# Differential values and gates as two token-major units of half products

## The chip, the cores and the metric

One of the eight cores of a Trainium2 chip runs the kernel. The number that counts is the device time of one launch in microseconds (us), here the median of three runs. The engines of a core work from their own instruction streams and meet by semaphores: TensorE (PE in the profile) multiplies into PSUM banks of 128 partitions x 512 fp32 values, VectorE (DVE) and ScalarE (ACT) do elementwise work, GpSimd (POOL) and SyncE (SP) mainly issue DMAs here.

## The reference

Two layers over 512 tokens of width 2048, all in float32. This change lies in the second one, which projects the normed x once and shares the columns out to an MLA branch and a differential attention branch:

```
z = rmsnorm(x, g) @ w_in
c_q, c_kv, k_rope, mla_gate, dq, dk, dv, diff_gate = split_cols(z, ODD_SPLITS)   # dv, diff_gate: 1024 each
...
a = p[:, 0] - lam * p[:, 1]                      # two causal softmaxes of one head, 8 heads
od = einsum("bhqk,bkhd->bqhd", a, vd)            # 128 values a head
od = rmsnorm(od, subln) * (1.0 - DIFF_LAMBDA_INIT)
y_d = od.reshape(B, S, DIFF_WIDTH) * jax.nn.silu(diff_gate)
return jnp.concatenate([y_c, y_d], axis=-1) @ w_out
```

## The kernel before

Matrices are multiplied in fp32r, each operand split into a high and a low part: `mm3` issues three matmuls (high x high, high x low, low x high) into one bank. A *row tile* is 128 of the 2048 rows of the contraction, so a job over 16 row tiles is 48 matmuls of 128x512.

Activations lie feature-major: `X1[k]` is the pair (high `sh`, low `sl`) of 128 features x 512 tokens of x times the gain g, made one by one as layer 0's output projection delivers them (`sink0`, which also writes x to `x1d` in HBM). The factor of the rms norm belongs to a token; it is put on when a sum leaves its bank (`evac`, a VectorE product with `rstd`), and the norm `n1` is finished only after the last row tile.

A weight `Piece` is 128 x 1024 floats (512 KB): SP loads it into one of three `wr` slots, ScalarE makes its high part (`wh`), VectorE its low part (`wl`), three slots each. `Piece.want()` is called as TensorE's row reaches a piece and sees to it that the splits of two pieces ahead and the loads of two more are issued. `big_job(wt, m, X, done, pre, norm)` is a job of two pieces into one bank of the pair "mm". The bank pairs "o", "sc" and "pt" serve attention outputs, scores and transposes.

The order on TensorE, ScalarE and VectorE is fixed when the program is built: `Plan` keeps a clock by a cost model, the jobs run in the order in which they were made, and after every step `tick` runs the side tasks (generators with a due time) that are due, which drops their instructions between the matmuls. Each engine works its row in order. SP's and GpSimd's rows follow from the framework's scheduler.

After layer 0 come eight heads of four jobs, `dq`, `dk`, `dv`, `dg` (tiles 4h to 4h+3 of `w1`), then five MLA gate jobs, the latents, the rope key, three more gates, the MLA heads and the output projection. `diff(h)` starts when `dv` has left its bank: it transposes v to token-major by four TensorE transposes (`pt<-cc,dv`), copies it out on ScalarE, and runs scores, softmaxes (`p`), transposes of them (`aT`) and `o`. `diff_gate` puts Silu on the gate, transposes the normed output `osb` and multiplies the two. x's tiles, scores, splits of activations and so on live in a pool of 76 work tiles of 128x512.

Of the kernel before, what the change touches and what calls it, by code (L numbers as in the profile page):

```python
# [9 lines left out]
F32 = mybir.dt.float32  # L10
# [63 lines left out]
class Plan:  # L74
# [82 lines left out]
    def after(self, *aps):  # L157

        return max(self.ready.get(a.tensor.name, 0.0) for a in aps)
# [30 lines left out]


@with_exitstack
def trunk_kernel(ctx: ExitStack, tc, xT, w0, w0o, wg, w1, wuq, wuk, wuv, w1o, small, cst, outT):
    plan = Plan()
    nc = tc.nc
    pe = Engine(plan, "PE", nc.tensor, plan.pe_cost)
# [86 lines left out]
    class Piece:  # L283


        def __init__(self, src, n, kept=False):
# [28 lines left out]
        def want(self):  # L315
            last = len(pieces) - 1
            while state["split"] <= min(self.i + 2, last):
                while state["dma"] <= min(state["split"] + 2, last):
                    pieces[state["dma"]].load()
                    state["dma"] += 1  # L320
                pieces[state["split"]].split()
                state["split"] += 1

        def get(self, off, n):
            h, l = self.parts[off // S]
            return h[:, off % S : off % S + n], l[:, off % S : off % S + n]

    jobs = []

# [608 lines left out]
        yield after(aT)  # L938
        out.append(aT)

    ods = {}

    def diff(h, st):
        t = []
        yield after(st["v"])
        yield from take("pt", t)
        transposes(t[0], st["v"], range(NB))
        yield after(t[0])
        v = wk("v")
        act.activation(v, t[0], AF.Copy)  # L950
        give("pt", t[0])
        q, kt, klow = st["q"], st["kh"], st["kl"]
        st.clear()
# [53 lines left out]
        ods[h] = osb  # L1007

    def diff_gate(h, z):
        while h not in ods:  # L1010
            yield plan.now + 0.5
        act.activation(z, z, AF.Silu)
        osb = ods.pop(h)
        yield after(osb)
        t = []
        yield from take("pt", t)
        transposes(t[0], osb, range(NB))
        yield after(t[0], z)
        dve.scalar_tensor_tensor(z, z, subs, t[0], ALU.mult, ALU.mult)
        give("pt", t[0])  # L1020
        Y1[h] = z

    def diff_jobs(h):
        st = {}

        def q_done(acc):
            z = evac(acc, n1, "dq")
            st["q"] = []
            plan.spawn(stacks(z, st["q"]))

        def k_done(acc):
            z = evac(acc, n1, "dk")
            lo = [wk("kl", F32R), wk("kl", F32R)]
            a = [wk("kh", F32R), wk("kh", F32R)]
            st["kh"], st["kl"] = a, lo

            def f():
                yield after(z)
                for c in range(2):
                    r, s = slice(64 * c, 64 * c + 64), slice(64 - 64 * c, 128 - 64 * c)  # L1040
                    high(a[c][r], z[r])
                    high(a[c][s], z[r])
                    yield after(a[c])
                    low(lo[c][r], z[r], a[c][r])
                    low(lo[c][s], z[r], a[c][r])
            plan.spawn(f())

        def v_done(acc):
            st["v"] = evac(acc, n1, "dv")
            plan.spawn(diff(h, st))  # L1050

        def g_done(acc):
            plan.spawn(diff_gate(h, evac(acc, n1, "dg")))
# [6 lines left out]
    for h in range(8):  # L1060
        diff_jobs(h)

    MG = [None] * 8

    def mla_gate_job(h):
        def done(acc):
            z = evac(acc, n1, "mg")

            def f():
                yield after(z)  # L1070
                act.activation(z, z, AF.Silu)
                MG[h] = z
            plan.spawn(f())
        big_job(w1, 32 + h, X1, done, None, n1)

    class Latent:
        def __init__(self, base, n, gcol):
# [41 lines left out]
            KR.extend((h, l))  # L1119
        plan.spawn(f())  # L1120

    for h in range(5):
        mla_gate_job(h)
    LQ = Latent(45, 6, C_QN)
    LKV = Latent(41, 4, C_KVN)
    big_job(w1, 40, X1, rope_key_done, None, n1)
    for h in range(5, 8):
        mla_gate_job(h)

    qrs = {}  # L1130
    VC = {}
# [49 lines left out]
    def mla(h, st):  # L1181
        while h not in qrs or not KR or "q" not in st or "k" not in st or h != started[0] or (h // 4, NB - 1) not in VC:
            yield plan.now + 0.4
        q, k, qr = st["q"], st["k"], qrs.pop(h)
        st.clear()
        vc = slice((h % 4) * P, (h % 4 + 1) * P)
        v = [VC[h // 4, n] for n in range(NB)]
        o = []
# [190 lines left out]
def _tiles1():  # L1379

    cq, ckv, kr, mg, dq, dk, dv, dg = 0, 768, 1280, 1344, 2368, 3392, 4416, 5440
    out = []
    for h in range(8):
        for b in (dq, dk, dv, dg):
            out.append(_ranges((b + 128 * h, b + 128 * h + 128)))
    for h in range(8):
        out.append(_ranges((mg + 128 * h, mg + 128 * h + 128)))
    out.append(_ranges((kr, kr + 64), (kr, kr + 64)))
    for j in range(4):
        out.append(_ranges((ckv + 128 * j, ckv + 128 * j + 128)))  # L1390
    for j in range(6):
        out.append(_ranges((cq + 128 * j, cq + 128 * j + 128)))
    return out


def _pack(w, tiles, rows=None):
# [7 lines left out]
    return out  # L1404


def _pack_small(w, cols):
# [80 lines left out]
```

## Time and profile before

| | |
|---|---|
| runs | 1565.23, 1565.57, 1565.69 us; median 1565.57 |
| profiled execution | 1567.61 us; its span in the trace 1565.8 us; granted TensorE clock 0.995 |
| busy | TensorE 1549.5 us, VectorE 866.4, ScalarE 705.2, GpSimd 48.2 |
| HBM | 146.49 MB read, 8.39 MB written, 99 GB/s over the span |

Nearly all instructions are recorded at line 62, the wrapper that also feeds the planner's clock, so groups are told apart by the names of the tiles: `mm<-sh,wh` is a matmul into a bank of the pair mm from a high part of x and a high part of a weight; `wl<-wr,wh` is the low part of a weight. "Idle before, releaser" is the engine's own idle time ahead of such instructions and what ended it. In the chain of work that ended last, pieces of one engine follow each other, and what waits for nothing is put to the engine itself.

### The profile page before, as it was taken

To read this page: it belongs to the slowest core of one execution; us is meant where nothing else is said; L and a number is where in the kernel's file an instruction comes from. 1 tells how busy PE (TensorE), PEld (TensorE's weight loads), DVE (VectorE), ACT (ScalarE), POOL (GpSimd) and SP (SyncE) were. 2 spreads that over 40 slices of the span, in tenths; PEclk is the share of its full clock that TensorE was granted. 3 is DMA by queue.
4 is the path that set the end of the run, shared out by engine and by line. 5 is a ranking of instruction groups with operands and counts; after the bars stand their busy time and mean duration, and the time that the engine had idled before them with its cause. 6 is when DMAs were issued, how large, how long until landed. Compare 5 with 4: busy or idle time off the path is not lost.

```text
span 1565.8 us, 19224 instructions
## 1 busy us (share of the span) xinstructions
PE 1549.5 (99%) x7450; PEld 1297.9 (83%) x7450; DVE 866.4 (55%) x1603; ACT 705.2 (45%) x1219; POOL 48.2 (3%) x76
## 2 busy tenths in 40 slices
PE   9999999999999999999999999999999999999996
PEld 7888888888888888888888888888888888888886
DVE  6877676677854344455445555543444465843344
ACT  6465555556643233444445444432323466632222
POOL 0000000000001010000000000000000000010000
PEclk9999999999999999999999999999999999999998
DMA  7223222322244443222222222222232221343323
GB/s 281 84 85 93 86 84 86 97 81 81 95 128 148 135 155 110 91 83 84 90 82 81 81 81 84 92 81 94 95 94 87 78 79 53 115 141 95 101 89 108
DMA packets 48922, 156.11 MB, mean 100 GB/s; under 512 B 5552, under 2 KB 9792, under 8 KB 48704
## 3 DMA queue, kind: packets, MB, share of 16 engines
q1 hardware_dynamic: 44576, 141.25, 28.4%
q0 software_dynamic: 4256, 13.64, 2.7%
q8 instruction: 58, 0.95, 0.3%
q14 instruction: 32, 0.26, 0.1%
HBM read 146.49 MB, written 8.39 MB: 99 GB/s over the span
## 4 chain that ended last, share of the span: by engine, by line
PE 97%; issue 1%; DVE 1%; DMA 0%; SPq 0%; POOLq 0%; ACT 0%; POOL 0%; DVEq 0%
PE mm L62 84%; PE o L62 5%; PE sc L62 5%; PE pt L62 4%; DMA xin<-in_xT 0%; DVE st L62 0%; SPq L62 0%; DVE sl L62 0%; POOLq L1483 0%; ACT sh L62 0%; POOL rcf L62 0%; DVE mg L62 0%; DVE yl L62 0%; DVE dg L62 0%; DVEq L1483 0%
## 5 line engine op out<-in xcount | busy, mean ns | idle before, releaser
L62 PE MATMUL mm<-sh,wh 128*128 128x512 f32 x1312 | 522.5, 398 | 0.0
L62 DVE TENSOR_TENSOR wl<-wr,wh 128x1024 fp32r<-128x1024 f32 (+1 forms) x244 | 290.6, 1192 | 418.3 <-ACT wh L62 418.2
L62 PE MATMUL mm<-sh,wl 128*128 128x512 f32 x1312 | 512.3, 390 | 0.0
L62 PE MATMUL mm<-sl,wh 128*128 128x512 f32 x1312 | 512.0, 390 | 0.0
L62 ACT ACTIVATE wh<-wr 128x1024 fp32r<-128x1024 f32 (+1 forms) x244 | 252.3, 1034 | 402.7 <-PE mm L62 325.1
L62 PEld LDWEIGHTS mm<-sh,wl 128*128 128x128 f32 x1312 | 246.3, 188 | 53.2
L62 PEld LDWEIGHTS mm<-sh,wh 128*128 128x128 f32 x1312 | 246.7, 188 | 45.3
L62 PEld LDWEIGHTS mm<-sl,wh 128*128 128x128 f32 x1312 | 247.1, 188 | 44.7
L62 PE MATMUL mm<-yh,wh 128*128 128x512 f32 x448 | 174.9, 390 | 0.0
L62 PE MATMUL mm<-yl,wh 128*128 128x512 f32 x448 | 174.5, 389 | 0.0
L62 PE MATMUL mm<-yh,wl 128*128 128x512 f32 x448 | 174.4, 389 | 0.0
L62 DVE CUSTOM_DVE_ANT_0 p<-sc,cc 128x128 f32<-128x128 f32 (+3 forms) x96 | 47.0, 490 | 96.6 <-PE sc L62 96.4
L62 PEld LDWEIGHTS mm<-yh,wl 128*128 128x128 f32 x448 | 84.1, 188 | 17.6
L62 PEld LDWEIGHTS mm<-yl,wh 128*128 128x128 f32 x448 | 84.1, 188 | 17.4 <-DVE yl L62 0.3
L62 PEld LDWEIGHTS mm<-yh,wh 128*128 128x128 f32 x448 | 84.1, 188 | 17.1
L62 ACT ACTIVATE p<-p,negm 128x128 f32<-128x128 f32 (+3 forms) x96 | 53.7, 560 | 68.3 <-DVE negm L62 66.8
L62 ACT ACT_TABLE_LOAD x50 | 64.2, 1283 | 1.5 <-PEq L1479 0.7
L62 ACT ACTIVATE aT<-pt 128x128 f32<-128x128 f32 (+3 forms) x64 | 27.7, 436 | 60.1 <-PE pt L62 59.9
L62 ACT ACTIVATE sq<-xr 128x512 f32<-128x512 f32 (+1 forms) x33 | 19.3, 586 | 55.0 <-DVE xr L62 55.0
L62 DVE TENSOR_TENSOR ss<-ss,sq 128x512 f32<-128x512 f32 (+1 forms) x54 | 36.1, 669 | 10.2 <-ACT sq L62 9.4
L62 PE MATMUL mm<-ch,wh 128*128 128x512 f32 x104 | 41.6, 400 | 0.0
L62 PE MATMUL mm<-cl,wh 128*128 128x512 f32 x104 | 40.6, 391 | 0.0
(253 smaller groups left out, 1822.0 us busy)
## 6 DMA issues: line engine op xcount, KB each, us to landing
wr<-in_w SPq DMA_DIRECT2D x166, 512.0 KB, 3.5
wr<-in_w0o SPq DMA_DIRECT2D x32, 512.0 KB, 3.6
wr<-in_w1o SPq DMA_DIRECT2D x32, 512.0 KB, 3.5
wr<-in_wuq SPq DMA_DIRECT2D x12, 384.0 KB, 3.1
xin<-in_xT SPq DMA_DIRECT2D x16, 256.0 KB, 5.2
xr<-in_xT POOLq DMA_DIRECT2D x16, 256.0 KB, 3.8
x1d<-xr POOLq DMA_DIRECT2D x16, 256.0 KB, 3.5
xr<-x1d POOLq DMA_DIRECT2D x16, 256.0 KB, 3.0
```

Of the source, the lines that this page charges most:

```text
L62: return f(*args, **kw)
```

## The change

`dv` and `dg` are no longer jobs of the heads. Each of the two column ranges of 1024 becomes a `Unit`, which computes the whole 512 tokens x 1024 columns token-major: blocks of 128 tokens of x stand still, weights move 512 wide, and a bank holds 128 tokens x 512 columns. Six pairs of row tiles (k and 8+k, twelve of sixteen) are multiplied by seven products of halves, after Strassen in Winograd's form: tokens are halved (256), row tiles are halved by the pairing, columns are halved (512). The sums of x (`T1` to `T4`) are made once by `differences()` from x read back from `x1d`; the sums of weights are made per piece by the class `Sum`, which loads one or two sources, adds on VectorE and then splits. Banks X, Y, Z are the pairs mm, o, sc, two token blocks each. Per pair of row tiles `differences()` issues two fetches by SP, two scalings and two high parts on ScalarE, five half-width differences and two low parts on VectorE. A piece holds two row tiles of one column half. After the first nine pieces (`first`) s1 is copied from X, then s2 = Z + s1 and s3 = Y + s2 are added; `second` lets Z and Y be written anew, `third` makes t = X - s3, `fourth` sends off c11 = Z + s1 and c12 = Y + s3, and the end c21 = X - s2 and c22 = Z + t. The four results leave by a ScalarE scaling with the token's norm factor (Identity for v, Silu for the gate) and a GpSimd DMA to `vd` and `gd` in HBM. The remaining four row tiles are multiplied plainly into the same banks by four ordinary pieces.

The order now is five MLA gate jobs (their results too go through HBM, `mgd`), unit v, unit g, then eight heads of `dq` and `dk` only, which fetch v and g by DMA as `dq` begins; then latents, rope key, three gates and the MLA heads as before. `diff` needs no transposing of v, puts the gate on with the norm (`osb`), and writes y from the transposed output on ScalarE. By the rows TensorE issues 696 matmuls of 128x512 for the two units where 768 stood for the sixteen jobs.

```
+    class Sum(Piece):
+        ahead = 3
...
+        def split(self):
+            vals = self.vals + [o.vals[0] for o in self.others]
+            if len(vals) > 1:
+                out = [wk("ws"), wk("ws")] if self.into is None else vals[self.into]
...
+                    for k in range(2):
+                        dve.tensor_tensor(out[k], vals[0][k], vals[1][k], ALU.add)
...
+                high(h[:, c], v[k])
+                low(l[:, c], v[k], h[:, c])
...
     def diff(h, st):
-        t = []
-        yield after(st["v"])
-        yield from take("pt", t)
-        transposes(t[0], st["v"], range(NB))
-        yield after(t[0])
-        v = wk("v")
-        act.activation(v, t[0], AF.Copy)
-        give("pt", t[0])
-        q, kt, klow = st["q"], st["kh"], st["kl"]
+        q, kt, klow, v, gate = (st[x] for x in ("q", "kh", "kl", "v", "g"))
...
-            dve.tensor_scalar(osb[:, c], o[:, c], ssq[:, n : n + 1], None, ALU.mult)
+            dve.scalar_tensor_tensor(osb[:, c], o[:, c], ssq[:, n : n + 1], gate[:, c], ALU.mult, ALU.mult)
...
-        act.activation(z, z, AF.Silu)
...
-        dve.scalar_tensor_tensor(z, z, subs, t[0], ALU.mult, ALU.mult)
+        y = wk("y")
+        act.activation(y, t[0], AF.Identity, scale=subs)
...
+        def fetch():
+            for x, src in (("v", vd), ("g", gd)):
+                st[x] = wk(x)
+                pool.dma_start(st[x], src[h])
...
-        big_job(w1, 4 * h, X1, q_done, None, n1)
-        big_job(w1, 4 * h + 1, X1, k_done, None, n1)
-        big_job(w1, 4 * h + 2, X1, v_done, None, n1)
-        big_job(w1, 4 * h + 3, X1, g_done, None, n1)
+        big_job(w1, 2 * h, X1, q_done, fetch, n1)
+        big_job(w1, 2 * h + 1, X1, k_done, None, n1)
...
+    NT = 6
+    def differences():
...
+    class Unit:
+        def __init__(self, wt, sink):
...
+            for i in range(n):
+                p1 = Sum([W(0, 0, i)])
+                p5 = Sum([W(1, 0, i), W(1, 1, i)], wide=False)
+                p6 = Sum([], (p5, p1), None)
+                seq += [(p1, "X", "B11", i), (p5, "Y", "T1", i), (p6, "Z", "T2", i)]
+            seq.append(self.first)
+            for i in range(n):
+                seq.append((Sum([W(0, 0, i), W(1, 0, i)], (), 1), "X", "T3", i))
+                if i < 2:
+                    if i == 0:
+                        seq.append(self.second)
+                    seq.append((Piece(W(0, i, 3), 1024), "ZY", None, i))
+            seq.append(self.third)
+            for i in range(n):
+                p2 = Sum([W(0, 1, i)])
+                p3 = Sum([], (self.keep[i], p2), 0)
+                seq += [(p2, "Z", "B21", i), (p3, "Y", "B22", i)]
+            seq.append(self.fourth)
+            for i in range(n):
+                seq.append((Sum([W(1, 1, i)], (), 0, i % 2 == 0), "X", "T4", i))
+            seq.append(self.fifth)
+            for i in range(2):
+                seq.append((Piece(W(1, i, 3), 1024), "XZ", None, i))
...
+    for h in range(5):
+        mla_gate_job(h, True)
+    Unit(w1u[0], away(vd, AF.Identity))
+    Unit(w1u[1], away(gd, AF.Silu))
+    for h in range(8):
+        diff_jobs(h)
```

TensorE in a differential head, before: the four transposes of v stand between the matmuls of the `dg` job, ahead of the head's scores.

```order
L62 MATMUL mm_994_5283<-sl_840_4285,wh_984_5211 128x512
L62 MATMUL mm_994_5283<-sh_839_4284,wl_985_5213 128x512
L62 MATMUL pt_999_5307<-cc_2_78,dv_998_5293 128x128 x4
L62 MATMUL mm_994_5283<-sh_850_4356,wh_984_5211 128x512
L62 MATMUL mm_994_5283<-sl_851_4357,wh_984_5211 128x512
L62 MATMUL mm_994_5283<-sh_850_4356,wl_985_5213 128x512
L62 MATMUL mm_994_5283<-sh_861_4428,wh_984_5211 128x512
```

The same engine in a head after: between the matmuls of `dq` or `dk` (`mm_1392` is one of these) stand scores of one head, the transposes of the output `osb` of another and output products (`o`) of a third, and no row transposes v.

```order
L62 MATMUL mm_1392_7368<-sh_948_5005,wl_1376_7292 128x512
L62 MATMUL sc_1421_7494<-kh_1400_7385,qa_1369_7249 128x256
L62 MATMUL sc_1421_7494<-kl_1398_7383,qa_1369_7249 128x256
L62 MATMUL pt_1424_7500<-cc_2_78,osb_1415_7469 128x128 x4
L62 MATMUL o_1344_7178<-v_1282_6906,aT_1423_7498 128x128 x3
L62 MATMUL sc_1426_7512<-kh_1401_7386,qb_1370_7250 128x256
L62 MATMUL sc_1426_7512<-kl_1399_7384,qb_1370_7250 128x256
```

The transposes of v are gone, and attention work of several heads is mixed. VectorE around the `dv` job, before: low parts of weights (`wl`), the last head's `osb` and gate product, and the eviction of `dv`.

```order
L62 TENSOR_SCALAR ssq_1002_5321<-ssq_1002_5321 128x4
L62 TENSOR_TENSOR kl_1062_5601<-dk_1060_5598,kh_1064_5603 64x512 x2
L62 TENSOR_SCALAR osb_1069_5643<-o_1001_5320,ssq_1002_5321 128x128 x4
L62 TENSOR_TENSOR wl_1073_5661<-wr_1054_5548,wh_1072_5659 128x1024
L62 SCALAR_TENSOR_TENSOR dg_1023_5398<-dg_1023_5398,subs_92_361,pt_1070_5652 128x512
L62 TENSOR_TENSOR wl_1077_5693<-wr_1066_5605,wh_1076_5691 128x1024
L62 TENSOR_TENSOR dv_1078_5698<-mm_1065_5604,rstd_971_5137 128x512
L62 ISA p_1086_5732,negm_1083_5727<-sc_1085_5729,cc_2_78 128x128
```

VectorE in unit v, after the first nine pieces: the low part of a plain piece, a sum of two loads and its low parts (`wx`, `wl_1109`), then the four additions that empty the banks sc (Z) and o (Y).

```order
L62 TENSOR_TENSOR wl_1104_5746<-wr_1087_5666,wh_1103_5744 128x1024
L62 TENSOR_TENSOR wx_1091_5690<-wr_1090_5688,wx_1091_5690 128x512
L62 TENSOR_TENSOR wx_1092_5691<-wr_1090_5688,wx_1092_5691 128x512
L62 TENSOR_TENSOR wl_1109_5769<-wx_1091_5690,wh_1108_5768 128x512
L62 TENSOR_TENSOR wl_1109_5769<-wx_1092_5691,wh_1108_5768 128x512
L62 TENSOR_TENSOR s2_1110_5780<-sc_1070_5592,s1_1105_5760 128x512
L62 TENSOR_TENSOR s3_1111_5788<-o_1065_5571,s2_1110_5780 128x512
L62 TENSOR_TENSOR s2_1112_5790<-sc_1071_5593,s1_1106_5762 128x512
L62 TENSOR_TENSOR s3_1113_5792<-o_1066_5572,s2_1112_5790 128x512
```

The additions stand behind the split of a piece that is used only later. TensorE in the same place of unit v: the end of the first `T3` piece in the banks mm, and the first plain piece, which begins anew in the banks sc that those additions read.

```order
L62 MATMUL mm_1055_5538<-wh_1098_5720,tl_991_5201 128x512
L62 MATMUL mm_1056_5539<-wh_1098_5720,th_988_5185 128x512
L62 MATMUL mm_1056_5539<-wl_1099_5721,th_988_5185 128x512
L62 MATMUL mm_1056_5539<-wh_1098_5720,tl_991_5201 128x512
L62 MATMUL sc_1070_5592<-wh_1103_5744,sh_861_4431 128x512
L62 MATMUL sc_1070_5592<-wl_1104_5746,sh_861_4431 128x512
L62 MATMUL sc_1070_5592<-wh_1103_5744,sl_862_4432 128x512
L62 MATMUL sc_1071_5593<-wh_1103_5744,sh_861_4431 128x512
```

Where a job had one bank for 48 matmuls, the bank now changes every three, and sc is written again one piece after its last product.

More of the change, by code (lines that the diff above doesn't have):

```diff
@@ L317, in want @@
             while state["split"] <= min(self.i + 2, last):
-                while state["dma"] <= min(state["split"] + 2, last):
+                while state["dma"] <= min(state["split"] + self.ahead, last):
                     pieces[state["dma"]].load()
@@ L1071, in f @@
                 act.activation(z, z, AF.Silu)
-                MG[h] = z
-            plan.spawn(f())
-        big_job(w1, 32 + h, X1, done, None, n1)
+                if away:
+                    yield after(z)
+                    pool.dma_start(mgd[h], z)
+                else:
+                    MG[h] = z
+            plan.spawn(f())
+        j = big_job(w1, 16 + h, X1, done, None, n1)
+        if h == 0:
+            j.pre = lambda: plan.spawn(differences())
+    NT = 6
+    TS = [None] * NT
@@ new lines, in differences, with fetch @@
+    def differences():
+        A, B = slice(0, 256), slice(256, 512)
+        def fetch(k):
+            xa, xb = wk("xa"), wk("xb")
+            sync.dma_start(xa, x1d[k])
+            sync.dma_start(xb, x1d[8 + k])
+            return xa, xb
+        nxt = fetch(0)
+        for k in range(NT):
+            xa, xb = nxt
+            if k + 1 < NT:
+                nxt = fetch(k + 1)
+            yield after(xa, xb)
+            act.activation(xa, xa, AF.Identity, scale=col(C_G1 + k))
+            act.activation(xb, xb, AF.Identity, scale=col(C_G1 + 8 + k))
+            yield after(xa, xb)
+            t13, t42 = wk("ta"), wk("tb")
+            dve.tensor_tensor(t13[:, A], xa[:, A], xa[:, B], ALU.subtract)
+            dve.tensor_tensor(t42[:, A], xb[:, A], xb[:, B], ALU.subtract)
+            dve.tensor_tensor(t13[:, B], xa[:, B], xb[:, B], ALU.subtract)
+            dve.tensor_tensor(t42[:, A], t42[:, A], t13[:, A], ALU.subtract)
+            dve.scalar_tensor_tensor(t42[:, B], t13[:, A], -1.0, xb[:, B], ALU.mult, ALU.subtract)
+            yield after(t42)
+            r = []
+            for t in (t13, t42):
+                h = wk("th", F32R)
+                high(h, t)
+                r.append(h)
+            yield after(*r)
+            for i, t in enumerate((t13, t42)):
+                l = wk("tl", F32R)
+                low(l, t, r[i])
+                r[i] = r[i], l
+            TS[k] = r
@@ new lines, in trunk_kernel, with operand, run, order @@
+    class Unit:
+        def __init__(self, wt, sink):
+            self.wt, self.sink, self.pre = wt, sink, None
+            W = lambda m, kh, i: wt[m, kh, i]
+            n = NT // 2
+            seq = []
+            self.keep = []
+            for i in range(n):
+                p1 = Sum([W(0, 0, i)])
+                p5 = Sum([W(1, 0, i), W(1, 1, i)], wide=False)
+                p6 = Sum([], (p5, p1), None)
+                self.keep.append(p6)
+                seq += [(p1, "X", "B11", i), (p5, "Y", "T1", i), (p6, "Z", "T2", i)]
[17 more added lines that the diff above has]
+                seq.append((Piece(W(1, i, 3), 1024), "XZ", None, i))
+            self.seq = seq
+            jobs.append(self)
+        def operand(self, name, k, b):
+            c = slice(b * P, b * P + P)
+            d = slice(256 + b * P, 256 + b * P + P)
+            if name == "B11":
+                x = X1[k], c
+            elif name == "B21":
+                x = X1[8 + k], c
+            elif name == "B22":
+                x = X1[8 + k], d
+            else:
+                plan.until(lambda: TS[k] is not None)
+                x = TS[k][name in ("T2", "T4")], c if name in ("T1", "T4") else d
+            (h, l), c = x
+            return h[:, c], l[:, c]
+        def run(self):
+            if self.pre:
+                self.pre()
+            self.banks = {}
+            self.tags = {}
+            self.begun = set()
+            self.done = set()
+            self.vals = {x: [None] * 2 for x in ("s1", "s2", "s3", "t", "c11", "c12", "c21", "c22")}
+            for s in self.seq:
+                if callable(s):
+                    s()
+                    continue
+                pc, where, name, i = s
+                for x, tag in zip("XYZ", self.order()):
+                    if x in where and x not in self.banks:
+                        plan.until(lambda: len(banks[tag]) == 2)
+                        self.banks[x], self.tags[x] = [bank(tag), bank(tag)], tag
+                pc.want()
+                for j in range(2):
+                    if name:
+                        todo = [(where, b, self.operand(name, 2 * i + j, b)) for b in range(2)]
+                    else:
+                        k = 8 * i + 6 + j
+                        plan.until(lambda: X1[k] is not None)
+                        todo = [(where[n // 2], n % 2, tuple(p[:, n * P : n * P + P] for p in X1[k])) for n in range(4)]
+                    for x, b, (xh, xl) in todo:
+                        out = self.banks[x][b]
+                        mm3(out, xh, xl, pc.get(j * S, S), (x, b) not in self.begun, False)
+                        self.begun.add((x, b))
+                    plan.tick()
+            self.last()
+            plan.tick()
+        def order(self):
+            return ("mm", "o", "sc")
+        def steps(self, name, *ops):
+            def f():
+                for b in range(2):
+                    for op in ops:
+                        yield from op(b)
+                self.done.add(name)
+            plan.spawn(f())
+        def wait(self, *names):
+            plan.until(lambda: all(x in self.done for x in names))
+        def combine(self, out, x, y, op, sign=ALU.add):
+            def f(b):
+                p, q = self.banks[x][b], self.vals[y][b]
+                yield after(p, q)
+                r = q if op else wk(out)
+                dve.tensor_tensor(r, p, q, sign)
+                self.vals[out][b] = r
+            return f
+        def leave(self, out, m, tokens):
+            def f(b):
+                z = self.vals[out][b]
+                plan.spawn(self.sink(m, 2 * tokens + b, z))
+                yield plan.now
+            return f
+        def free(self, x):
+            def f(b):
+                give(self.tags[x], self.banks[x][b])
+                yield plan.now
+            return f
+        def first(self):
+            def copy(b):
+                p = self.banks["X"][b]
+                yield after(p)
+                self.vals["s1"][b] = wk("s1")
+                act.activation(self.vals["s1"][b], p, AF.Copy)
+            self.steps("s1", copy)
+            self.wait("s1")
+            self.begun -= {("X", 0), ("X", 1)}
+            self.steps("s3", self.combine("s2", "Z", "s1", False), self.combine("s3", "Y", "s2", False))
+        def second(self):
+            self.wait("s3")
+            self.begun -= {("Z", 0), ("Z", 1), ("Y", 0), ("Y", 1)}
+        def third(self):
+            self.steps("t", self.combine("t", "X", "s3", False, ALU.subtract))
+        def fourth(self):
+            self.wait("t")
+            self.steps("top", self.combine("c11", "Z", "s1", True), self.leave("c11", 0, 0),
+                       self.combine("c12", "Y", "s3", True), self.leave("c12", 0, 1), self.free("Y"))
+        def fifth(self):
+            self.wait("top")
+            self.begun -= {("Z", 0), ("Z", 1)}
+        def last(self):
+            self.steps("end", self.combine("c21", "X", "s2", True, ALU.subtract), self.free("X"),
+                       self.leave("c21", 1, 0), self.combine("c22", "Z", "t", True), self.free("Z"),
+                       self.leave("c22", 1, 1))
```

79 lines of the change are left out of this document (54 added, 25 removed).

## The prediction

> **What bounds the kernel now.** I read the head of the page first, then the chain of work that ended last.
>
> ```profile
> span 1565.8 us, 19224 instructions
> PE 1549.5 (99%) x7450; PEld 1297.9 (83%) x7450; DVE 866.4 (55%) x1603; ACT 705.2 (45%) x1219; POOL 48.2 (3%) x76
> PE 97%; issue 1%; DVE 1%; DMA 0%; SPq 0%; POOLq 0%; ACT 0%; POOL 0%; DVEq 0%
> ```
>
> TensorE is busy in all of the span and is 97% of the chain, so time goes away only where TensorE gets fewer instructions, and comes back only where it has to wait. The profiled run took 1567.61 us for this span; the median of the runs shown is 1565.57 (1565.23 to 1565.69), 2.04 lower. I sum against 1567.6 and take 2.0 off at the end. Next the chain in two windows, for the pace of TensorE at the turn of the layers and for one differential head:
>
> ```profile
> 554.88 61.43 PE mm L62 x271
> ...
> 647.69 0.44 PE pt L62 x4
> ...
> 649.51 0.24 PE sc L62 x2
> ...
> 689.16 0.44 PE pt L62 x4
> ...
> 698.46 0.44 PE pt L62 x4
> ```
>
> The first row is the pace: 61.43/271 = 0.2267 us for one 128x512 matmul. 647.69 is the transposing of one head's v (four blocks, 0.44 us), and 698.46 the next head's: a head takes 50.77 us, of which four jobs of 48 matmuls are 43.53, the v transposes 0.44 and its attention and output transposes the other 6.80. 649.51 is the head's first score and 689.16 the transposing of its finished output, 39.7 us later. Then windows, to see whether that pace depends on who else works:
>
> ```profile
> 12.00:16.00 4.00, 4.00 (x13) 3.13 (x13) 3.83 (x6) 4.00 (x8) 0.00 (x0) 0.66 1.05 404
> 0.00:20.00 20.00, 16.23 (x62) 12.97 (x63) 11.57 (x19) 13.37 (x22) 2.06 (x8) 0.91 0.92 336
> 20.00:40.00 20.00, 20.00 (x90) 16.57 (x89) 15.80 (x32) 14.33 (x27) 0.00 (x0) 1.00 0.56 213
> 360.00:380.00 20.00, 20.00 (x94) 16.68 (x93) 19.18 (x30) 11.03 (x19) 0.00 (x0) 1.00 0.29 85
> 620.00:1040.00 420.00, 420.00 (x2028) 350.33 (x2028) 218.30 (x449) 196.44 (x374) 10.55 (x7) 1.00 0.27 84
> 1240.00:1300.00 60.00, 60.00 (x322) 51.68 (x321) 35.36 (x86) 36.01 (x74) 0.00 (x0) 1.00 0.22 65
> ```
>
> The columns after the window are its length and the busy time of TensorE, its weight loads, VectorE, ScalarE and GpSimd, then the granted clock, the DMA share and GB/s. At 360 VectorE is busy for 19.18 of 20 us and TensorE still is for all 20. At 20 two accumulators take turns every few matmuls, and at 1240 blocks of the activations stand still while weights move 512 wide, the two habits of the new units: TensorE stays full and its clock 1.00. So form and company cost nothing by themselves. Last, what TensorE waits for, three rows of six, 6.7 us in all; the first lies in the first 30 us, the second at the very end, and the third is the only one between 200 and 1440 us:
>
> ```profile
> PE o L62 <- ACT sh L62: 2.1, 2, 1.3
> PE pt L62 <- DVE dg L62: 1.8, 1, 1.8
> ...
> PE mm L62 <- DVE yl L62: 0.3, 1, 0.3
> ```
>
> **What the change removes.** Sixteen jobs of 48 matmuls go (768). A unit has 6 pairs of row tiles × 7 products × 2 token blocks × 3 split products = 252 matmuls, and 4 plain row tiles × 2 column halves × 4 token blocks × 3 = 96, so 348; two units are 696. All are 128x512. 72 fewer at 0.2267 us: −16.3 us. Eight times four v transposes at 0.44: −3.5 us. Together −19.8 us on the path. (The Trainium skill, TensorE: Matmul & The Clock Gate, section Back-to-back issue gap, gives N/2.4 + 2.5 ns for an isolated gap, which is 216 ns for 512 columns and an estimate of 15.5 us for the 72, and a sustained 131 ns, by which they would be worth 9.4 us; the row's 227 ns is near the first and no row here shows the second.)
>
> **What it adds on VectorE and ScalarE**, with prices from groups kept apart by form:
>
> ```profile
> L62 DVE TENSOR_TENSOR wl<-wr,wh 128x1024 fp32r<-128x1024 f32 x224 | 273.6, 1222 | 392.5 <-ACT wh L62 392.3
> L62 ACT ACTIVATE wh<-wr 128x1024 fp32r<-128x1024 f32 x224 | 237.2, 1059 | 391.1 <-PE mm L62 316.5 <-issue 70.3 <-ACT pr L62 0.9
> L62 DVE TENSOR_TENSOR wl<-wr,wh 128x512 fp32r<-128x512 f32 x8 | 5.5, 691 | 4.4 <-ACT wh L62 4.4
> L62 ACT ACTIVATE wh<-wr 128x512 fp32r<-128x512 f32 x8 | 5.0, 626 | 2.7 <-PE mm L62 1.9 <-ACT wh L62 0.8
> L62 DVE TENSOR_TENSOR dv<-mm,rstd 128x512 f32<-128x512 f32 x8 | 5.5, 683 | 0.0
> L62 DVE TENSOR_TENSOR st<-xr,pt 128x256 f32<-128x256 f32 x15 | 5.1, 414 | 0.7 <-PE pt L62 0.7
> L62 ACT ACTIVATE sh<-xr,sm 128x512 fp32r<-128x512 f32 x16 | 11.6, 725 | 30.3 <-DVE xr L62 30.3
> L62 ACT ACT_TABLE_LOAD x50 | 64.2, 1283 | 1.5 <-PEq L1479 0.7
> ```
>
> *Differences of x, beside the five gate jobs.* 12 scalings at 0.725 and 12 high parts at 0.626 are 16.2 us on ScalarE; 30 half-width differences at 0.414 and 12 low parts at 0.69 are 20.7 us on VectorE. The five jobs are 240 × 0.2267 = 54.4 us of TensorE and need 5 × (2 × 1.222 + 0.683) = 15.6 us of VectorE: 36 of 54 us, so they hide. But the first gate job cannot be evicted before the norm of layer 1 is finished, and its last sums now share VectorE and ScalarE with the differences. I take 0.4 us, between nothing and twice a 0.725 scaling, 1.5.
>
> *Inside a unit, feeding.* A weight piece gives 12 matmuls, 2.72 us, in the sums. Three of them (a plain half, a sum of two loads, a sum of sums) are 8.16 us of TensorE and 1.22 + 2 × (2 × 0.69 + 2 × 0.69) = 6.74 us of VectorE, 83%, and 1.06 + 4 × 0.63 = 3.6 of ScalarE. A split may begin when the piece three before is used up, 5.44 us ahead of its use, and by these durations ends about 3 us ahead. That is cover, and the 360 row says a VectorE at 96% still feeds. Cost 0. If that cover goes, each of some 25 pieces a unit is late by what is missing.
>
> *Inside a unit, the turn.* After the last of the first nine pieces (call that T) TensorE does the next, 2.72 us, in X and then wants Z's and Y's banks, which VectorE must first add up into s2 and s3. Ahead of these in VectorE's row stand the two low parts of the next sum, whose high part waits for a slot that comes free at T: 0.63 + hop, so the low parts end at about T+2.05, the first s2 at T+2.7, and at the back-to-back 0.63 to 0.69 the second s2 at T+4.0. TensorE has Z's first block at T+2.8 and 0.68 us of work in it, then waits to T+4.05: 0.7 to 0.85 us lost. I take 0.85, ends 0.2 (the low parts come early) and 2 (a piece of 1.22 us or a late load stands there too). Two units: 1.7. Queued behind the s2 and s3 is the split of the next plain piece, needed only one piece later. The other waits (copies of s1 on ScalarE, t, the upper quadrants) each have at least one piece of 2.72 us or more ahead of their use: 0.
>
> *Entry and boundary.* The first unit needs both "mm" banks, and one holds the last gate's sum: 0.68 us of matmuls in the first cover an eviction of 0.683 and its hops nearly: 0.3, ends 0 and 1.5 (a 1.22 split ahead of it). Between the units the same banks wait on c21, two additions of which one lies under the last matmuls: 0.35, ends 0 and 1.
>
> *Through HBM.* v and g are written by GpSimd and read back by head:
>
> ```profile
> x1d<-xr POOLq DMA_DIRECT2D x16, 256.0 KB, 3.5
> xr<-x1d POOLq DMA_DIRECT2D x16, 256.0 KB, 3.0
> wr<-in_w SPq DMA_DIRECT2D x166, 512.0 KB, 3.5
> xin<-in_xT SPq DMA_DIRECT2D x16, 256.0 KB, 5.2
> ```
>
> 3.5 + 3.0 us after the last unit (the write goes in 512-byte runs now; twice as long would do as well); head 0 first uses v after two jobs, 21.8 us. Hidden. What would wait on GpSimd behind a write that itself waits for its scaling is the next write alone. On SP a unit moves 25 times 512 KB in 348 × 0.2267 = 79 us: 166 GB/s, where the first 20 us show 336. SP issues in order and a load waits for its slot; the least room that I find from issue to use is 5.7 us, in the last two pieces, against 3.5. Cost 0.
>
> *The heads after.* 50.77 − 2 × 10.88 − 0.44 = 28.57 us each. VectorE had 218.30/420 × 50.77 = 26.4 us a head and loses four splits (4.89), two evictions (1.37) and the gate product (0.74): some 19.6, 69%. ScalarE had 23.7 and loses four high parts (4.24), a gate's Silu and a copy (1.2) and two table loads (2.57): about 15.7. The chain of 39.7 us now covers 1.4 heads; two "o" banks allow 2 × 28.57 = 57. Attention work is 24% of TensorE's row instead of 13%, with fewer matmuls between two dependent steps. I take 1.0 us for all eight, ends 0 and 6 (0.75 each, little over one eviction of 0.683).
>
> **Sum.** −19.8 + 0.4 + 0.3 + 1.7 + 0.35 + 1.0 = −16.0. 1567.6 − 16.0 = 1551.6 for the profiled run, 1549.6 for the median. All low ends: 0.4 us of cost, 1546.2; all high ends: 1.5 + 1.5 + 4 + 1 + 6 = 14, 1559.8.
>
> **The rivals.**
> - *All hidden.* Only 0 to 1 us of waits: 1546. For it: 420 us with TensorE busy in all of them, VectorE full or not. Against it: the turn, which by durations cannot be under the matmuls there are.
> - *Dearer turns.* The additions stand behind a whole sum (2.76) and a split (1.22), so each of the two turns costs some 3 us more: 1549.6 + 6 = 1556. For it: VectorE works in a fixed order that a cost model set, 83% full there.
> - *The heads become chain-bound.* If the chain of 39.7 us grows to 60 as two heads share VectorE, 60/2 = 30.0 instead of 28.57 a head: +11.4, 1561. Decides from 57 us on. Against: VectorE falls to 69%.
> - *Slower: loads come late.* One mechanism: SP's queue in the units, where a sum loads two pieces. The row of 5.2 us for 256 KB in the crowded start shows that landing can stretch. From 5.7 us on loads are late; at 7 us about ten a unit are late by up to 3.5 us, 20 × 1.75 = 35: 1585. The gain is used up at 0.8 us over for each of twenty, 6.5 us.
> - *Slower: the clock.* At 12 us, after TensorE had waited for its first data, the clock is 0.66 and 13 matmuls take 4.00 us. If waits at the turns brought the units, 158 us, to a clock of 0.9, that is 17.5 us and the gain is gone: 1567; at 0.8, 39 us: 1589. Against: the turns that I expect are under 2 us, and the waits of up to 1.3 us on sh, in the first 30 us, did not keep the clock from 1.00 in the row of 20 us. [...]
>
> **How the numbers follow.** Forecast 0.45; all hidden 0.15; dearer turns 0.20; chain-bound heads 0.09; loads late by enough to be slower 0.05; the clock 0.02; 0.04 for loads or chain that eat the gain nearly. A measurement of this kernel tells 0.2%, 3.1 us, from no change: faster is below 1562.4, slower above 1568.7. So faster 0.45 + 0.15 + 0.20 + 0.09 = 0.89, same 0.04, slower 0.07. The range takes in the first three cases and all the bounds: 1544.5 (somewhat under the 1545.8 of no cost at all, for the spread of runs) to 1560.
>
> **What the profile after would show.** Heads with a period of 28.6 us and no pt from dv; the units as 79 us each of matmuls at 0.2267, broken by one wait on s2 or s3 of under 1 us; TensorE waits of some 10 us in all instead of 6.7; clock 1.00. Waits of TensorE on wh, wl or a weight DMA inside the units would show the feeding wrong; waits on aT or sc in the heads, the chain; a landing over 5.7 us, the loads. The forecast is wrong if any of these repeats per piece and not per unit.

## The result, and the profile after

The changed kernel takes 1547.15 us (median of four runs, 1547.10 to 1548.18) where the kernel before, beside it, takes 1565.63 (1565.23 to 1566.98): ratio 0.9882, 95% interval 0.9865 to 0.9899, 18.5 us less. The forecast was 1549.6 in a range of 1544.5 to 1560. The page of the changed kernel, against the one before:

```profile
span 1545.4 us, 19462 instructions
PE 1529.6 (99%) x7346; PEld 1280.0 (83%) x7346; DVE 935.6 (61%) x1741; ACT 728.6 (47%) x1285; POOL 71.3 (5%) x118
PE 96%; issue 2%; DVE 1%; DMA 0%; ACT 0%; SPq 0%; POOLq 0%; POOL 0%; DVEq 0%; ACTq 0%
```

VectorE has 69 us more to do and ScalarE 23, and TensorE, busy for 99% as before, has 104 records fewer (72 matmuls and 32 transposes): the span follows the row of the engine that bounds it. The spans differ by 20.4 us and the medians by 18.5, since the profiled run before was some 2 us above its median. Its first 20 us show where: there TensorE had a clock of 0.91 and 62 matmul records. In the run after, the windows (columns as in the prediction) read

```profile
0.00:20.00 20.00, 18.08 (x72) 13.80 (x73) 12.76 (x21) 14.66 (x24) 2.07 (x8) 1.00 0.93 344
20.00:40.00 20.00, 20.00 (x90) 16.57 (x89) 16.82 (x42) 14.33 (x26) 0.00 (x0) 1.00 0.64 226
660.00:840.00 180.00, 178.57 (x781) 145.95 (x780) 113.70 (x157) 72.11 (x101) 15.80 (x23) 1.00 0.54 176
850.00:1070.00 220.00, 220.00 (x1124) 185.77 (x1123) 150.15 (x372) 127.67 (x299) 12.16 (x16) 1.00 0.28 88
```

The first row has 72 records, at 1.00. The change does not reach that place, and the medians are what counts. The third row lies in the units, the fourth in the heads, where TensorE is busy in all 220 us. What TensorE waits for (us in total, times, longest) is 5.8 us in six rows, against 6.7 before; those that matter:

```profile
PE pt L62 <- DVE dg L62: 1.8, 1, 1.8
PE sc L62 <- DVE s L62: 1.3, 4, 0.4
...
PE mm L62 <- DVE yl L62: 0.3, 1, 0.3
```

One row is new, the second: four waits on s2, two in each unit, where the prediction put its turn. The chain shows the first of the two turns (start, us, what):

```profile
688.29 0.69 DVE wx L62
...
689.09 0.64 ACT wh L62
...
689.76 1.29 DVE wl L62 x2
691.05 0.61 DVE s L62
...
691.69 1.30 DVE s L62 x2
...
693.03 0.96 PE sc L62 x3
693.99 1.39 PE o L62 x6
695.38 1.36 PE sc L62 x6
```

It is the order of VectorE's row that was listed with the change: the sum's two additions (`wx`), its high part, its low parts (`wl`), then s2, s3, s2, and TensorE goes on in sc as the second s2 is done. The reader should also see the 0.96 us for three matmuls, which at the pace of 0.2267 are 0.68. TensorE's own rows in that place tell where the rest comes from (start, length of the record, in brackets the idle time before it):

```profile
691.02 0.39 PE L62 MATMUL mm<-wh,tl 128*128 128x512 f32 x1
691.71 0.50 PE L62 MATMUL sc<-wh,sh 128*128 128x512 f32 x1 [0.29 <-DVE s L62]
692.04 0.40 PE L62 MATMUL sc<-wl,sh 128*128 128x512 f32 x1
692.28 0.39 PE L62 MATMUL sc<-wh,sl 128*128 128x512 f32 x1
693.03 0.50 PE L62 MATMUL sc<-wh,sh 128*128 128x512 f32 x1 [0.36 <-DVE s L62]
693.36 0.39 PE L62 MATMUL sc<-wl,sh 128*128 128x512 f32 x1
```

In a stream a record lasts 0.39 us and the next starts 0.2267 us after it, so neighbours overlap by 0.16 us. A wait takes that overlap away, and the matmul behind it lasts 0.50 us, with the next one 0.33 us later instead of 0.23. From start to start a wait thus costs some 0.27 us more than the row of waits says.

The window of 660 to 840 us is a good ruler from here on, since TensorE has 128x512 matmuls alone there: at 0.2267 us it has room for 794. The changed kernel gets 781 in, so 13 × 0.2267 = 2.9 us are lost in the units: 1.43 us in which TensorE is not busy, and about as much in restarts. Counted from start to start, the trace has these losses at four places and nowhere else: 0.38 us at the entry (664.56), 1.20 at each of the two turns, 0.29 at the boundary between the units (745.04), 3.1 in all.

### The profile page after: what moved, and what is told of

It is laid out like the page before. It is cut to its first block, busy times and chain, and to the rows that moved or that the text cites. A ratio compares the mean times of both kernels' runs of the same rounds, so it can differ in the third digit from the quotient of the medians.

```text
span 1545.4 us, 19462 instructions
## 1 busy us (share of the span) xinstructions
PE 1529.6 (99%) x7346; PEld 1280.0 (83%) x7346; DVE 935.6 (61%) x1741; ACT 728.6 (47%) x1285; POOL 71.3 (5%) x118
## 4 chain that ended last, share of the span: by engine, by line
PE 96%; issue 2%; DVE 1%; DMA 0%; ACT 0%; SPq 0%; POOLq 0%; POOL 0%; DVEq 0%; ACTq 0%
PE mm L62 78%; PE sc L62 8%; PE o L62 7%; PE pt L62 3%; DMA xin<-in_xT 0%; DVE st L62 0%; ACT wh L62 0%; DVE s L62 0%; SPq L62 0%; DVE wl L62 0%; DVE sl L62 0%; DVE mg L62 0%; DVE wx L62 0%; POOLq L1736 0%; ACT sh L62 0%
## 5 line engine op out<-in xcount | busy, mean ns | idle before, releaser
L62 DVE TENSOR_TENSOR wl<-wr,wh 128x1024 fp32r<-128x1024 f32 (+1 forms) x236 | 280.9, 1190 | 379.1 <-ACT wh L62 374.7
L62 PE MATMUL mm<-sh,wh 128*128 128x512 f32 x1056 | 419.4, 397 | 0.0
L62 ACT ACTIVATE wh<-wr 128x1024 fp32r<-128x1024 f32 (+1 forms) x236 | 243.8, 1033 | 360.7 <-PE mm L62 252.7
L62 PE MATMUL mm<-sl,wh 128*128 128x512 f32 x1056 | 412.1, 390 | 0.0
L62 PE MATMUL mm<-sh,wl 128*128 128x512 f32 x1056 | 412.1, 390 | 0.0
L62 PEld LDWEIGHTS mm<-sh,wl 128*128 128x128 f32 x1056 | 198.2, 188 | 42.8
L62 PEld LDWEIGHTS mm<-sh,wh 128*128 128x128 f32 x1056 | 198.6, 188 | 36.1
L62 PEld LDWEIGHTS mm<-sl,wh 128*128 128x128 f32 x1056 | 198.8, 188 | 35.5
```

The costliest lines, as they stand in the source:

```text
L62: return f(*args, **kw)
```

## The experiments

**The yardstick**, the changed kernel once more:

> The changed kernel itself, as the yardstick on this chip for the runs beside it. Every theory: 1547.2 us, 18.4 under the kernel before.

It took 1547.3 us (ratio 0.9885, 0.9870 to 0.9900) beside 1565.39 for the kernel before; the runs below are held against this. Where they ran on other chips, the kernel before took 1565.44 to 1565.52 beside them, so chips differ by little.

**Units without half products.** All eight pieces of each column half are plain, and the banks leave by a copy:

```
-                p1 = Sum([W(0, 0, i)])
...
+            for m, where in ((0, "ZY"), (1, "XZ")):
+                for kh in range(2):
+                    for i in range(4):
+                        seq.append((Piece(W(m, kh, i), 1024), where, None, (kh, i)))
```

> Both units stay token-major, with the same order, the same way through HBM and the same heads, but all sixteen row tiles are multiplied plainly (no differences of x, no sums of weights, 768 matmuls for the two units as in the sixteen jobs of the kernel before). Theory A, the time follows TensorE's row: of the gain only the v transposes are left, 8 x 0.44 = 3.5 us, less some tenths at the banks that are written anew: 1562.2 to 1563. Rival B, the gain came from relief elsewhere (fewer table loads, less VectorE and ScalarE work in the heads, longer overlap of heads): most of it stays, under 1555.

1561.42 us on the same chip, 4.0 under the kernel before (ratio 0.9974, 0.9964 to 0.9984); it was to be 1562.2 to 1563. Theory A stands against rival B: of the 18.1 us that the change gives, 14.1 are the half products. Its window:

```profile
660.00:840.00 180.00, 179.63 (x792) 148.14 (x791) 50.26 (x49) 43.93 (x47) 10.85 (x15) 1.00 0.37 116
```

792 matmuls, 0.5 us lost, with 50 us of VectorE instead of 114. So the half products save 16.3 us of matmuls and lose 2.9 − 0.5 = 2.4 more than plain pieces: 13.9, against 14.1 measured.

**Fewer half products.** Two pairs of pieces through the products instead of three:

```
-    NT = 6
+    NT = 4
```

> Eight of sixteen row tiles through the seven products, eight plainly: 24 matmuls more. Theory A: 5.4 us more, turns as before, 1552.7. Rival C: less work on VectorE gives some of it back, 1550 or less.

1553.37 us (0.9924, 0.9909 to 0.9939), 6.1 over the yardstick where 5.4 were due, with 1.4 us of waits on s. It goes by the count of matmuls; VectorE's relief gives nothing back. The other way, all sixteen row tiles through the products (24 matmuls fewer, expected at 1539.9 us), there is no time: that program deadlocks. So no run shows whether the sums still feed TensorE with no plain piece among them.

**The transposes of v alone**, left out of the kernel before:

```
-        yield from take("pt", t)
-        transposes(t[0], st["v"], range(NB))
...
-        act.activation(v, t[0], AF.Copy)
+        act.activation(v, st["v"], AF.Copy)
```

> The kernel before with one thing left out: the four transposes of v a head (v is copied as it left its bank, so the attention output is another one; the copy and all else stay). The prediction's step: 8 x 0.44 = 3.5 us less, 1562.0. Theory A' (the plain units gained 4.0 us net of 0.5 us of losses of their own, so a head without its transposes is worth 0.13 us more than they): 4.5 us less, 1561.0. Rival B (they lie beside other work): 1565.

1561.85 us beside 1565.52 (0.9977, 0.9968 to 0.9986): 3.7 us, nearer to the prediction's 3.5 than to the 4.5 of A', which its interval (2.2 to 5.0 us) does not exclude; rival B is excluded. The plain units' gain was 4.0 net of 0.5 lost in them, so by the medians 0.8 us of it would be from something else in the heads. That is less than the intervals of the two runs allow for, so it may be nothing; no run here tells.

**The turn, with more cover and with none.** The first plain piece one piece later, or one earlier:

```
-                if i < 2:
-                    if i == 0:
+                if i > 0:
+                    if i == 1:
                         seq.append(self.second)
-                    seq.append((Piece(W(0, i, 3), 1024), "ZY", None, i))
+                    seq.append((Piece(W(0, i - 1, 3), 1024), "ZY", None, i - 1))
```

> The first plain piece of each unit stands after the second T3 piece instead of after the first, so the additions that free Z and Y have 5.44 us of matmuls over them instead of 2.72. Theory A (the 1.3 us of waits on s at the two turns are VectorE's row against a cover of one piece): the waits fall to 0.2 or less and the time by 1.1 to 1.3, to 1546.0. Rival C (the wait is a fixed cost of going from additions to writing the bank): 1.3 us of waits and 1547.2 stay.

> The first plain piece stands before the first T3 piece: no matmuls over the additions. In VectorE's row they stand behind one sum only, which is made earlier. Theory A: TensorE waits from the end T of the ninth piece to T+0.85 for the first s2 and once more 0.6 for the second, 1.45 a turn instead of 0.66, so waits of 2.9 and 1548.8. If a turn cost whole splits (rival C', 3 us a turn): 1553.

Both missed. They took 1547.06 and 1547.20 us, the yardstick's time within its spread. With more cover the waits on s are 1.6 us, not 0.2; with none 1.3, not 2.9:

```profile
PE sc L62 <- DVE s L62: 1.6, 2, 0.8
```

(with more cover), and with none

```profile
PE sc L62 <- DVE s L62: 1.3, 4, 0.4
```

Taken alone this speaks for rival C, a fixed cost. The chain with more cover says otherwise:

```profile
691.46 0.68 DVE s L62
692.14 0.61 DVE wx L62
...
692.85 0.64 ACT wh L62
...
693.52 1.29 DVE wl L62 x2
694.81 1.21 DVE s L62 x2
...
696.07 0.96 PE sc L62 x3
```

The planner set the next sum (`wx`, `wl`, 2.7 us) between the first s2 and the rest: in the code each addition is a step of its own, and by this order one came due before the split and the others after. The cover was given back in VectorE's row. Without cover the first s2 started earlier than I had reckoned, at 688.21 us, just ahead of the ninth piece's last matmul (688.27): it needs the first token block alone, whose last matmul is 0.68 us ahead of the piece's end.

**The turn, with cover and order.** As with more cover, and

```
-            self.steps("s3", self.combine("s2", "Z", "s1", False), self.combine("s3", "Y", "s2", False))
+            def add():
+                yield after(*self.banks["Z"], *self.banks["Y"], *self.vals["s1"])
+                for out, x, y in (("s2", "Z", "s1"), ("s3", "Y", "s2")):
+                    for b in range(2):
+                        r = wk(out)
+                        dve.tensor_tensor(r, self.banks[x][b], self.vals[y][b], ALU.add)
...
-            return ("mm", "o", "sc")
+            return ("o", "mm", "sc") if self.wt is first_unit else ("mm", "o", "sc")
```

> The changed kernel with the first plain piece behind the second T3 piece, the four additions s2, s2, s3, s3 together in VectorE's row ahead of the next sum, and the first unit's X in the banks o instead of mm (so that neither entry nor boundary waits for an eviction). Theory A (of the 160.6 us that the units take for 696 matmuls 2.8 are lost where a bank is written anew, about 1.4 as waits and 1.4 as slow first matmuls behind them): the additions end at T+5.0 and the bank is wanted at T+5.44, no waits on s, the units take 158.3 and the time falls by 2 to 2.8 us, to 1544.5 to 1545.3. Rival C (writing a bank anew costs that in any order, as two orders with the same time suggest): 1547.

1544.19 us (1543.89 to 1544.20; ratio 0.9863, 0.9849 to 0.9876), 3.1 under the yardstick and the fastest kernel of this study. No wait on s is left in its list, and its window is full:

```profile
660.00:840.00 180.00, 180.00 (x796) 149.05 (x795) 115.14 (x158) 72.95 (x102) 16.32 (x24) 1.00 0.56 184
```

796 matmuls, nothing lost, with the same sums and 115 us of VectorE. That refutes rival C: the 3.1 us were where the additions stand in VectorE's row and which banks a unit begins with. By place, the 2.4 us of the turns went with cover and order together (cover alone left 2.2 of them) and the 0.7 of entry and boundary, which cover alone left as they were, with the banks. The order without the added cover was not run.

**VectorE's share.** Low parts of sums computed twice, in all sums or in those of two loaded halves:

```
                 low(l[:, c], v[k], h[:, c])
+                nc.vector.tensor_tensor(l[:, c], v[k], h[:, c].bitcast(F32), ALU.subtract)
```

> The same only for the sums that load two halves (T1, and one of three T4): 8.1 us of VectorE for 8.16 of TensorE, 99%. Theory A: still hidden, 0 to 1 us: 1547.3 to 1548.3. Rival E (a VectorE above some 90% makes TensorE wait piece by piece, 25 times 0.3): 1555.

> Every low part of a sum piece is computed twice (the same values into the same tile; the planner is not told, so every engine's order stays). VectorE then needs 10.5 us for three pieces that give TensorE 8.16. Theory A: VectorE feeds TensorE in the units and 100% is where it starts to cost: in the first nine pieces 3 x 2.4 less the lead of 3 us, some 4 us, 1.3 more at the turn, 1 to 2 in the B21 and B22 pieces: 6 to 7 a unit, about 1560 (1555 to 1566), with TensorE waiting for wl. Rival D (feeding has slack far beyond VectorE's share, or is held by loads): under 1550.

At 99% by durations it is 1548.32 us, 1.0 more, at the upper end of theory A. In the trace VectorE is busy for 7.40 and 7.57 of 8 us in the first nine pieces, 94%, and TensorE for all of them:

```profile
672.00:680.00 8.00, 8.00 (x37) 6.64 (x36) 7.40 (x12) 3.26 (x5) 0.00 (x0) 1.00 0.40 137
680.00:688.00 8.00, 8.00 (x37) 6.64 (x36) 7.57 (x13) 2.78 (x5) 0.00 (x0) 1.00 0.49 153
```

What it costs shows at the turns, where the waits on s are 1.9 us instead of 1.3. With all low parts twice, 129% by durations, it is 1570.99 us, slower than before (1.0038, 1.0024 to 1.0052) and 23.7 over the yardstick, where 13 were expected. The direction is theory A's, the size is not. Windows of that kernel (the first three where its clock fell), its waits, and the matmuls behind three of these:

```profile
692.00:696.00 4.00, 2.93 (x8) 2.32 (x9) 3.96 (x6) 1.80 (x4) 0.00 (x0) 0.70 0.40 133
700.00:704.00 4.00, 3.81 (x10) 2.58 (x10) 3.96 (x6) 0.00 (x0) 0.00 (x0) 0.57 0.05 7
792.00:796.00 4.00, 3.45 (x8) 2.57 (x9) 3.93 (x6) 0.00 (x0) 0.00 (x0) 0.57 0.22 91
660.00:840.00 180.00, 164.16 (x677) 127.91 (x676) 157.21 (x213) 63.01 (x91) 10.06 (x14) 0.97 0.44 142
```

```profile
PE sc L62 <- DVE s L62: 6.0, 3, 3.7
PE mm L62 <- ACT s L62: 3.6, 2, 1.8
PE sc L62 <- DVE wl L369: 3.1, 5, 1.0
PE mm L62 <- DVE wl L369: 2.7, 4, 0.7
```

```profile
693.07 0.50 PE L62 MATMUL mm<-wh,th 128*128 128x512 f32 x1 [1.83 <-ACT s L62]
699.77 0.50 PE L62 MATMUL sc<-wh,sh 128*128 128x512 f32 x1 [2.09 <-DVE s L62]
792.55 0.79 PE L62 MATMUL sc<-wh,sh 128*128 128x512 f32 x1 [3.70 <-DVE s L62]
```

677 of 794 matmuls, 26.5 us lost, 23.6 more than in the yardstick: all of it is in the units. The waits listed are 15.4 us. About 5 us more are the clock, 0.97 over the 180 us: it fell at waits of 1.83, 2.09 and 3.70 us, and matmuls started 0.43 us apart instead of 0.23 for some 3.4 us each time. Restarts at 0.27 us for 14 waits make 3.8. Why the waits are so long has two links that I had left out, both from a late VectorE. The sums free their slots later, so SP issues the loads later, as its timeline shows:

```profile
665.55 0.33 SPq L62 DMA_DIRECT2D wr<-in_w1u  x1
...
676.21 0.33 SPq L62 DMA_DIRECT2D wr<-in_w1u  x1
...
686.86 0.33 SPq L62 DMA_DIRECT2D wr<-in_w1u  x1
```

These are 10.7 us apart where in the changed kernel it is 7.5 and 8.2. And TensorE waits for copies on ScalarE (`ACT s`, 3.6 us). How much of the waits is due to each was not separated.

**Loads.** One attempt, copying each source once more from HBM to HBM, tested something else:

```
+                nc.sync.dma_start(spare[spared[0]], src)
```

> Every source that a sum piece loads is copied once more by SP from HBM to an unused place in HBM: 42 x 512 KB more read and as much written in the two units, about 166 + 2 x 139 GB/s. The prediction's rival of late loads: landing grows from 3.9 us to more than 5.7 and TensorE waits for wl or wh, 5 us or more in the units: 1552 or above. Theory A (slots, not landing, set when a load starts, and there are 5.7 us or more to its use): landing 4.5 to 5.5 us, 1547.3 to 1548.5.

1557.48 us, as rival and not theory, but not in the units: their loads landed in 3.6 and 4.7 us, and the window has 782 matmuls. SP's order, which the framework sets, had put the copies, which wait for nothing, into the first 110 us, where TensorE now waited 6.2 us for the first norm (`ss`):

```profile
40.00:60.00 20.00, 13.77 (x56) 11.29 (x55) 12.83 (x39) 5.56 (x8) 1.03 (x1) 0.82 1.00 356
60.00:80.00 20.00, 20.00 (x84) 16.14 (x84) 14.74 (x23) 9.83 (x15) 0.60 (x1) 0.93 0.83 302
```

So the loads of the units were made late in another way, by issuing each wide one twice into its slot:

```
                     t = self.slot("wr", F32)
+                    nc.sync.dma_start(t, src)
                     sync.dma_start(t, src)
```

> Every 512 KB load of a sum piece in the units is issued twice into the same slot, and the second waits until the first has landed: a wr tile is there some 7.5 us after its first issue instead of 3.9, and SP stands still for 3.5 us each time, 11 times a unit. (The copies to HBM in another run did not test this, since SP's order put them into the first 110 us.) The prediction's rival of late loads: from 5.7 us on they are late, at 7 us twenty loads by 1.75 us on average, all of it on the path: 35 us more, 1582. Theory A (by the trace the tightest loads have 5.9, 6.3 and 6.9 us from issue to first use and the others 7 to 18, and a split still has some 3 us of lead on TensorE): the few late loads are taken up by that lead, 0 to 3 us more, 1547.3 to 1550.

1550.93 us (0.9910, 0.9893 to 0.9926), 3.6 over the yardstick, a little above the bound of theory A and a tenth of the rival's 35. Where it shows is the turn, not each load:

```profile
PE sc L62 <- DVE s L62: 3.8, 4, 1.7
```

The additions stand behind a sum that now waits for its load. No wait on wl, wh or a load stands in its list: the other late loads were taken up by the lead of the splits.

**The heads in series.** A head takes its output bank only when the head before has given its own back:

```
+        while h and h - 1 not in oout:
+            yield plan.now + 0.2
         o = []
         yield from take("o", o)
```

> The changed kernel with the heads' attention in series: a head takes its output bank only when the one before has given its own back. The prediction's rival of chain-bound heads has a head's chain of 40 us or more take the place of 28.6 us: at least 8 x 11.4 = 91 us more, 1638. Theory F (no job waits for a head's attention: TensorE goes on with the next jobs, latents and gates, and the attention only has to be through when the second output projection starts, at 1309 us in the trace, 200 us behind the last head): within 1 us of 1547.3.

1548.20 us (0.9890, 0.9876 to 0.9903), 0.9 over the yardstick. The last head's output is now normed at 1185.5 us:

```profile
L62 DVE SCALAR_TENSOR_TENSOR osb<-o,ssq,g x32: 340/342/352, 900.1 to 1185.5; 128x128 f32<-128x128 f32 x32
```

instead of 1088.3 in the changed kernel, and TensorE loses nearly nothing, since the jobs do not wait for it.

## Why the prediction was right, step by step

- *The gain, −19.8 us.* Right in both parts: the transposes alone measured 3.7 (2.2 to 5.0) for 3.5, and the half products save what their 72 matmuls take, less what the units lose. That TensorE's row sets the time is shown by four kernels with 24 or 72 matmuls or 32 transposes between them.
- *The turn, 1.7 us for both units.* The place and the cause are right, the additions behind a sum in VectorE's row; the size is 2.4. The prediction had one wait a turn, on the second s2, and the trace has two: VectorE's row came some 0.3 us later, since the high part waited for the sum's second addition (`wx` ends at 688.98, `wh` starts at 689.09) and not for its slot, so the first s2 was late as well. And each wait costs 0.27 us more than its idle time, a term that the prediction did not have. Entry and boundary were put at 0.3 and 0.35 and are 0.38 and 0.29. What the prediction had not seen is that all of it depends on order and banks: with two pieces of cover, the additions side by side and other banks it is nothing.
- *Feeding, 0.* Right, and the condition as well: hidden with VectorE at 99% by durations (94% busy in the trace), not at 129%. The sentence on what happens when the cover goes (each piece late by what is missing) was too mild, since a late VectorE delays slots, loads and copies too.
- *Loads, 0.* Right in the changed kernel. The least room, put at 5.7 us, is 5.9 by the trace, but not where the text has it: the last two pieces of unit v have 10.0 and 9.2 us from issue to first use, and the tightest are the first load of the second unit (5.9) and two sums after the turn (6.3 and 6.9). The rival's price of 35 us was wrong: it put each late load on the path and forgot the 3 us of lead that the same text gives the splits.
- *The start of layer 1, 0.4 us.* No wait stands there after: the differences of x are hidden.
- *The heads, +1.0 us.* Not paid: TensorE is busy in all 220 us of the heads. Whether they even gain something (0.8 us by the medians) is open. VectorE is busy for 150.15 of these 220 us, 68% where the text had 69% (its 19.6 us a head should read 19.4; nothing hangs on it). The rival of chain-bound heads (0.09, 1561 us) did not come to pass, and not because the chain stayed short: head 0's runs from its first score at 855.9 us to the transposing of its output at 910.7, 54.8 us instead of 39.7. The fixed order lets jobs run on while the attention falls behind, and even with the heads in series it costs 0.9 us.
- *Together*: 16.3 for the matmuls and 3.7 for the transposes, less 3.1 in the units, is 16.9, against 18.1 on the same chip; the 1.2 us between them are within the intervals and not explained. The forecast was 2.45 us too high. It had 3.75 us of costs: the turns cost 0.7 more than it took, and the 1.4 for the start of layer 1 and the heads were not paid. That these two errors are of opposite sign is luck. TensorE's waits are 5.8 us in all, not the 10 that it looked for.
- *The clock.* The changed kernel's longest new wait is 0.4 us and the clock is 1.00 in the units, so that rival did not come to pass. That it is a real mechanism of this kernel two experiments show: about a wait of 6.2 us the granted clock was 0.82 and then 0.93 for 20 us each, and in the kernel with all low parts twice it fell at waits of 1.83, 2.09 and 3.70 us. It stayed at 1.00 at a wait of 1.80 us in that same kernel and at one of 1.71 us with the loads made late. The prediction's argument from the waits of up to 1.3 us on sh does not hold: in the kernel before they end at 9.3 us, ahead of the row of 0.66 at 12 us, and the row of 20 us only shows the clock after it had come back. So the length of one wait does not decide, and what does is not shown. The last of these waits:

```profile
9.32 0.51 PE L62 MATMUL o<-sh,sh 128*128 128x512 f32 x1 [1.31 <-ACT sh L62]
```

The Trainium skill, TensorE: Matmul & The Clock Gate, section HAM oscillation, gives as its rule that there be no idle gaps of TensorE over about 3.4 us. The waits of 3.70 and 6.2 us go with it, but the falls at 1.83 and 2.09 us do not, and in the first 12 us of the kernel before no wait is over 1.31 us; here the measurement decides, and shorter waits were enough.

## What to carry to other kernels

Where one engine is 97% of the chain, count its instructions at the pace of the trace and look for the few places where a bank it writes is still being read; the rest of a large rewrite can be free, here 69 us of VectorE work. At such a place look at what stands ahead of the emptying operations in the in-order row of the other engine: more cover did nothing as long as the planner put other work between them, and cover with the operations side by side took the turns' cost away. A count of matmuls in a window that holds nothing else measures such losses better than the list of waits, which leaves out the restart behind each wait.

## What the runs showed of the hardware

In a stream the records of 128x512 matmuls last 0.39 us and start 0.2267 us apart. Behind a wait of 0.3 us the first record lasts 0.50 us and the next starts 0.33 us after it, at a granted clock that reads 1.00, so from start to start a wait costs 0.27 us more than its idle time: four waits of 1.3 us in all cost 2.4. The clock fell, with matmuls 0.43 us apart for some 3.4 us, at waits of 1.83, 2.09 and 3.70 us, and stayed at 1.00 at waits of 1.71 and 1.80 us. And TensorE was busy for all of 16 us in which VectorE was busy for 94%, as long as nothing that it waits for stood behind the booked work.
